# Padding small tiles so that the weights and split tiles lie at 0, the parts' tiles at 64 modulo 128 bytes

## The chip, the cores and the metric

The kernel runs on one core of a Trainium2 chip. The metric is the device time of one execution in microseconds; the median of three executions before the change is 1647.09 us (1642.84 to 1648.29).

## What is computed

A four-layer encoder over 256 tokens of 1024 features in float32. Each layer is a mixer and an MLP, both added to x; the mixers are a bidirectional state-space scan (layers 0 and 3), a dilated attention (layer 1) and a differential attention (layer 2).

```
for i in range(4):
    h = rmsnorm(x, norm_mix_g[i])
    h = (ssd_mixer, dilated_mixer, diff_mixer)[i % 3](h, ...)
    x = x + h
    x = x + square(relu(rmsnorm(x, norm_mlp_g[i]) @ w1[i])) @ w2[i]
return rmsnorm(x, final_norm_g)
```

w1 is 1024x4096, w2 4096x1024; the mixers have products of the same kind.

## The kernel before, in words

**Activations** lie as [feature, token]: x is the tile xT, 8 blocks of 128 features by 256 tokens. A product holds a 128x128 block of weights stationary in the array and moves 256 tokens past it. To get float32 accuracy from the fast float32r format, both operands are split into a rounded part and a remainder, and each product is three passes (`mm3`, lines 143, 144, 145): high weights by high x, high weights by low x, low weights by high x. A few weight chunks of the scan mixer are used whole in float32 (line 141).

**Weights** come as a stream of chunks of 128x1024 in the order in which the parts plan them: a DMA on SP's queue into raw (5 buffers), a copy on ACT into whi (line 110), a subtraction on DVE into wlo (line 112; 5 buffers each). A chunk of three passes is 24 matmuls in the MLP.

**Moving operands** are of three kinds. The norm writes x times its gains, split, into the split tiles spl (`norm_split`, lines 226 and 227; the factor of the root mean square is put in after the product). The MLP's first products ("up", banks r0 to r3) and the first units of each mixer move spl; so do the output products of the mixers, whose inputs are split into spl tiles too. The MLP's second products ("down", banks a0 to a3) move hh and hl, the split square of the first products. The other input products of the mixers move nh and nl, the split normalised x (`normalised`). Only the differential mixer's v products have it the other way: nh and nl are stationary, whi and wlo move (lines 962 to 964); the dilated mixer's v products (lines 820 to 822) likewise with 384 columns.

**Memory.** Tiles are taken from pools in the order of their first use, each at a multiple of 32 bytes of every partition: const (head, vec, cst: inputs that stay; ones; the guards of the norms), xp (xT), wp (raw, whi, wlo), sp (spl, 12 buffers), small (`ap_`: the three tiles rs_y, rs_w and rs_q of the inverse root, two buffers each, then rbc, dg, sqacc, sq), and last the pool of the part that runs (`lp`), which begins anew with each part. So an odd size in an early pool moves all that lies behind it. Start addresses modulo 128 bytes, before and after:

| tiles | before | after |
|---|---|---|
| head | 0 | 0 |
| vec | 32 | 0 |
| cst, ones | 64 | 0 |
| xT | 32 | 0 |
| raw, whi, wlo | 32 | 0 |
| spl | 32 | 0 |
| rbc, dg, sqacc, sq | 96 | 64 |
| nh, nl, nf, hh, hl | 96 | 64 |
| scan mixer: z2, cvx, cvB, cvC, bc, e, G, xt | 32 | 64 |
| dilated mixer: q, S, PT, v | 32 | 64 |
| dilated mixer: k, by head pair | 0 or 32 | 64 |
| differential mixer: q, k, S, PT | 0 | 64 |

Rows of these tiles have sizes that are multiples of 128 bytes, so that every slice that a product uses begins at the same place modulo 128 as its tile.

**Order.** The program's order is worked out ahead of the run from priorities; the engines wait for one another by semaphores. The steps of the prediction lie in `mm3`, in `rsqrt` (lines 249 to 261), in `load` (guards, lines 161 to 164), in `start` of the scan mixer (line 419: the halved gain of the skip, tile dh, read at line 620) and in the two attention mixers' small tiles (m, nm, ss, lamt, bias).

Of the kernel before, what the change touches and what calls it, by code (L numbers as in the profile page):

```python
# [10 lines left out]
F32 = mybir.dt.float32  # L11
F32R = mybir.dt.float32r
I32 = mybir.dt.int32
AF = mybir.ActivationFunctionType
ALU = mybir.AluOpType
PSUM = bass.MemoryType.PSUM
P = 128
T = 256
D = 1024
# [8 lines left out]
WARM = (8, 0, 4, 4, 4)  # L28


def classes(t):
    """Tokens j*4 + c of [.., 256] as [.., c, j]: the order of the dilated mixer."""
    return t.rearrange("p (j c) -> p c j", c=4)


class LayerPool:
    """The pool of the part that is being emitted."""
# [8 lines left out]
class Prog:  # L46
    def __init__(self, ctx, tc, aps, parts):
        self.ctx, self.tc, self.nc, self.a = ctx, tc, tc.nc, aps
        self.parts = parts
        ep = lambda name, bufs=1, **k: ctx.enter_context(tc.tile_pool(name=name, bufs=bufs, **k))  # L50
        self.const = ep("const")
        self.xp = ep("xp")
        self.wp = ep("wp")
        self.sp = ep("sp")
        self.ap_ = ep("small")
        self.lp = None
        self.dr = ep("dr", space=bass.MemoryType.DRAM)
        self.ps = ep("ps", space=PSUM)
        self.head = self.const.tile([P, aps["head"].shape[1]], F32, name="head")
        self.vec = self.const.tile([P, aps["vec"].shape[1]], F32, name="vec")  # L60
        self.cst = self.const.tile([P, aps["cst"].shape[1]], F32, name="cst")
        self.plan = []
        self.rep, self.bvec = {}, None
        self.n_dma = self.n_conv = self.n_take = self.n_done = 0
        self.chunks = {}

    @contextmanager
    def shifted(self, name):
        """Emits with the priority of a later (or earlier) place in the program."""
        n = max(self.tune[name], -self.tc.cur_priority)  # L70
        self.tc.cur_priority += n
        yield
        self.tc.cur_priority -= n

# [5 lines left out]
    def plan_chunk(self, key, ap):  # L80
        """A key that ends in "f32" is used as it is, without a split."""
        self.plan.append((key, ap))
# [44 lines left out]
    def mm2(self, out, q, kh, kl, start):  # L127
        """The product of 64 rows: q holds hi above lo, kh twice the keys' hi."""
        mm = self.nc.tensor.matmul
        mm(out, lhsT=q, rhs=kh, start=start, stop=False, skip_group_check=True)  # L130
        mm(out, lhsT=q[0:64], rhs=kl, start=False, stop=True, skip_group_check=True)  # L131
# [16 lines left out]
    def load(self, g, perm):  # L148
        """x to [feature, token] with the first gains, what the first products need ahead of the other constants."""
# [10 lines left out]
        nc.vector.memset(self.ones, 1.0)  # L160
        self.guard = {}
        for n, v in ((1, EPS / P), (D, 1.0 / D), (8 * D, 0.125 / D)):
            self.guard[n] = self.const.tile([P, 1], F32, name=f"guard{n}")
            nc.vector.memset(self.guard[n], v)
# [84 lines left out]
    def rsqrt(self, v, n):  # L249
        """1/sqrt(v) for v [128, n] (the guard within): a seed of the bits and two Newton steps, each with the factors that even its error out."""  # L250
        nc = self.nc
        t = lambda nm, dt=F32: self.ap_.tile([P, n], dt, tag=f"rs_{nm}_{n}", name=f"rs_{nm}_{n}", bufs=2)
        y, w, q = t("y"), t("w"), t("q", I32)
        nc.vector.tensor_scalar(out=q, in0=v.bitcast(I32), scalar1=-0.5, scalar2=float(0x5F1FFFF9), op0=ALU.mult, op1=ALU.add)
        cur = q.bitcast(F32)
        for a, b in ((0.703952253 * 2.38924456, 0.703952253), (1.5 * (1 + 3.17e-7), 0.5 * (1 + 3.17e-7))):
            nc.vector.scalar_tensor_tensor(out=w, in0=cur, scalar=-b, in1=cur, op0=ALU.mult, op1=ALU.mult)
            nc.vector.tensor_tensor(out=w, in0=w, in1=v, op=ALU.mult)
            nc.vector.scalar_tensor_tensor(out=y, in0=w, scalar=a, in1=cur, op0=ALU.add, op1=ALU.mult)
            cur = y  # L260
        return y

    def sums(self, bank, tiles, count):
        """bank [128 tokens, 2 blocks] = sums over the features of each [128 features, 256 tokens] over count, and eps."""
        cols = [(self.ones, self.guard[1])] + [(t, self.guard[count]) for t in tiles]
        for i, (t, v) in enumerate(cols):
            for h in range(2):
                self.nc.tensor.matmul(bank[:, h:h + 1], lhsT=t[:, 0:P] if i == 0 else t[:, h * P:(h + 1) * P], rhs=v,
                                      start=i == 0 and h == 0, stop=i == len(cols) - 1, skip_group_check=True)

    def bcast_tok(self, r, scale, bank, out):
        """r [128 tokens, 2 blocks] times scale -> out [128, 256], the same on every partition."""
# [15 lines left out]
    def normalised(self, g_mix, perm=False, keep=False):  # L288
        """x*g/rms split, all of it."""
# [87 lines left out]
    def tail_chunks(self, key, w, k0, nk):  # L377
        """The last nk row blocks of an output product, cut by columns."""
# [3 lines left out]
    def proj_tail(self, acc, key, xs, finish, first=False):  # L382
        """The last row blocks of an output product, column block by column block."""
# [14 lines left out]
    def ssd_events(self, l, finish):  # L398
        """The layer as (time, weight chunks, emitter); a unit of time is one product of two column blocks."""
# [11 lines left out]
        def start():  # L411
            self.norm_finish("a0")
            st["n"] = self.normalised(gvec("g_mix", 8 * l, 8), keep=any(n[0] != "o" for n in cfg["native"]))
            # sums of squares of the gated y, two column blocks at a time
# [3 lines left out]
            st["dh"] = lp.tile([P, 16], F32, name="dh")  # L418
            nc.vector.tensor_scalar(out=st["dh"], in0=gvec("dskip", 16 * j, 16), scalar1=0.5, scalar2=None, op0=ALU.mult)
# [3 lines left out]
        def unit(kind, c0, defer):  # L423
            """Two column blocks of in_w from column c0; -> (bank, keys)."""
# [54 lines left out]
        # dt: softplus, its logarithm, sums along the tokens within the blocks of 128  # L479
# [12 lines left out]
        def dt_post():  # L492
# [24 lines left out]
            # ln(dt): a seed of the bits and Newton steps with exp  # L517
# [8 lines left out]
        def dt_sums():  # L526
            adt, ln = st["adt"], st["ln"]
            b = self.bank("r2")
            ge, le = self.C("tri_ge"), self.C("tri_le")  # [s, s']: 1 where s >= s', s <= s'
# [24 lines left out]
        def load_rows(g, i):  # L554
            """The rows of two heads on every partition."""
# [11 lines left out]
        def cb(g):  # L567
            b = self.bank("r2")
            B, C = st["B", g], st["C", g]
            for i in range(2):  # token blocks 1, 0  # L570
# [15 lines left out]
        def gh(g, i):  # L586
            """The decayed scores of two heads, [s, l] for both directions."""
            bc, tb = st["bc", g, i], st["tb"]
            X = lambda o, i_, bias: nc.scalar.activation(out=o, in_=i_, func=AF.Exp, bias=bias)  # L589
            # blocks of 128: [s1 l0 | s1 l1 | s0 l0 | s0 l1], then the forward diagonals of token blocks 1 and 0  # L590
# [15 lines left out]
        def y(g):  # L606
# [3 lines left out]
            # two heads in turn: they hold different columns of the array  # L610
# [40 lines left out]
        def r2():  # L651
            bank = self.bank("r2")
            # the sums are of 2y
# [52 lines left out]
    def bias_vectors(self):  # L706
        """[16 heads: by k-q from -256 | the same, far ones masked | by (k-q)/4 from -64 | the same, every fourth]."""
        nc, a = self.nc, self.a
        oh = self.lp.tile([32, 1280], F32, name="oh")
        tab = self.lp.tile([32, 16], F32, name="tab")  # L710
# [13 lines left out]
    def bias_rows(self):  # L724
        """Copies of the vectors one after another, of which a slanted pattern reads Toeplitz matrices."""
# [6 lines left out]
    def slanted(self, name, h, off, dims):  # L732
        """Row h of the vectors at off - step*i for each (step, count) of dims, and so on."""
# [4 lines left out]
    def split(self, hi, lo, src, scale):  # L738
        """hi + lo = src*scale, src in PSUM or SBUF."""
# [4 lines left out]
    def dil_events(self, l, finish):  # L744
# [9 lines left out]
        def start():  # L754
# [4 lines left out]
            for i in range(2):  # L759
                st["bias", i] = lp.tile([P, 2, 514], F32, name=f"bias{i}")  # L760
# [69 lines left out]
        def scores(hp, qb):  # L830
# [10 lines left out]
            m = lp.tile([P, 4], F32, tag="m", name="m", bufs=4)  # L841
# [11 lines left out]
            nm = lp.tile([P, 6], F32, tag="nm", name="nm", bufs=4)  # L853
# [18 lines left out]
        def pv(hp, qb):  # L872
            """The two heads in turn: they hold different columns of the array."""
# [46 lines left out]
    def diff_events(self, l, finish):  # L920
# [8 lines left out]
        def start():  # L929
            self.norm_finish("a0")  # L930
            st["n"] = self.normalised(self.V("g_mix", 8 * l, 8))
            # -lambda on every partition; the gain of the head norm with its factor
            t = lp.tile([P, 6], F32, name="lamt")
# [58 lines left out]
        def scores(h, qb):  # L992
# [5 lines left out]
            m = lp.tile([P, 6], F32, tag="m", name="m", bufs=4)  # L998
# [22 lines left out]
        def pv(h):  # L1021
            b = self.bank("a3")
            pt, v = st.pop(("PT", h)), st["v", h // 2]
            m = lp.tile([P, 2], F32, tag="ss", name="ss", bufs=2)
# [59 lines left out]
    def final_tile(self, n):  # L1084
        """A feature block of x*g, transposed."""
# [42 lines left out]
    def prepare_part(self, i):  # L1128
        """Plans the weights of a part; -> its emitter."""
# [49 lines left out]
def bucket(rel):  # L1179
    """The bucket of each distance (of the shapes alone)."""  # L1180
# [6 lines left out]
def prepare(nc, ins):  # L1187
    """The arrays of the launch: the inputs, laid out, and constants of the shapes alone."""
# [73 lines left out]
```

## Time and profile before

| | |
|---|---|
| runs | 1642.84, 1648.29, 1647.09 us; median 1647.09 |
| span of the profiled execution | 1641.6 us, 1.2 us under the fastest run |
| TensorE's granted clock, mean over the span | 0.991 |
| busy: PE, weight loads, DVE, ACT, POOL | 98%, 95%, 73%, 58%, 8% |
| DMA | 299.84 MB, mean 183 GB/s |
| first MLP | about 242 to 441 us of the span |

A row of the view of a line reads: line, engine, operation, out<-in by tile names (buffer numbers left out), count, then smallest, median and largest duration in ns, then the first and last start in us. A row of the grouped view has instead the busy time in us, the mean duration in ns, and the idle time of the engine before these instructions with what ended it. A row of the timeline is start and duration in us. A matmul's record is longer than the distance to the next one's start, since matmuls overlap in the array. Some matmul records are missing from a trace, a few per cent.

### The profile page before, as it was taken

The numbers are of one execution on the slowest core, as the hardware profiler recorded it, in microseconds if no ns is written. First come the engines' busy times: TensorE is split into PE (matmuls) and PEld (weight loads), VectorE is DVE, ScalarE is ACT, GpSimd is POOL, SyncE is SP. The second block draws the span as 40 slices with busy tenths as digits, with TensorE's granted clock in tenths as the row PEclk, the third lists the DMA queues.
The fourth block names the chain that finished last, engine by engine and source line by source line (L and its number), as shares of the span: only waits on it lengthen the run. The fifth ranks groups of instructions, "written<-read, shape, count | busy, mean of one in ns | idle before, by whom it ended". The sixth has DMA issues, their size and how long they took to land.

```text
span 1641.6 us, 32376 instructions
## 1 busy us (share of the span) xinstructions
PE 1612.2 (98%) x13018; PEld 1552.6 (95%) x13018; DVE 1198.2 (73%) x1996; ACT 959.9 (58%) x1627; POOL 129.2 (8%) x116
## 2 busy tenths in 40 slices
PE   8999999999999999999999999999999999999998
PEld 7989999999999999999999999999999899899997
DVE  7999997555776666666556888755579999985554
ACT  5577865444666666655445666644455778654443
POOL 0011121000200000010000000100010231210001
PEclk9999999999999999999999999999999999999999
DMA  6677765766475555546665554566655777656651
GB/s 208 209 217 231 224 191 180 218 212 185 134 198 166 151 157 154 161 134 186 190 192 182 184 174 120 166 192 188 187 160 178 218 218 224 217 169 191 187 188 64
DMA packets 230294, 299.84 MB, mean 183 GB/s; under 512 B 16496, under 2 KB 166256, under 8 KB 230144
## 3 DMA queue, kind: packets, MB, share of 16 engines
q1 hardware_dynamic: 209552, 262.51, 52.4%
q10 hardware_dynamic: 20592, 35.27, 7.6%
q8 instruction: 102, 1.67, 0.4%
q14 instruction: 48, 0.39, 0.1%
HBM read 296.41 MB, written 3.62 MB: 183 GB/s over the span
## 4 chain that ended last, share of the span: by engine, by line
PE 79%; DVE 11%; DMA 4%; ACT 3%; issue 2%; POOL 0%; SPq 0%; DVEq 0%; ACTq 0%; POOLq 0%
PE r L143 14%; PE r L145 13%; PE r L144 13%; PE a L143 8%; PE a L145 8%; PE a L144 8%; DVE wlo L112 3%; DMA bc<-scr 2%; DMA raw<-in_ssd_in_w_dram 2%; PE r L141 1%; PE a L820 1%; PE r L614 1%; PE a L822 1%; PE a L821 1%; PE r L131 1%
## 5 line engine op out<-in xcount | busy, mean ns | idle before, releaser
L112 DVE TENSOR_TENSOR wlo<-raw,whi 128x1024 fp32r<-128x1024 f32 (+1 forms) x490 | 593.8, 1219 | 304.7 <-ACT whi L110 303.3
L110 ACT CAST whi<-raw 128x1024 fp32r<-128x1024 f32 (+1 forms) x490 | 502.6, 1032 | 458.1 <-PE r L144 237.6
L145 PE MATMUL r<-spl,wlo 128*128 128x256 f32 x1248 | 356.6, 286 | 3.7 <-DVE wlo L112 3.7
L143 PE MATMUL r<-spl,whi 128*128 128x256 f32 x1248 | 357.4, 287 | 0.5 <-ACT whi L110 0.5
L144 PE MATMUL r<-spl,whi 128*128 128x256 f32 x1248 | 357.3, 286 | 0.3 <-DVE spl L227 0.3
L143 PE MATMUL r<-nh,whi 128*128 128x256 f32 (+1 forms) x1024 | 290.1, 283 | 3.9 <-DVE cvx L469 2.4
L145 PE MATMUL r<-nh,wlo 128*128 128x256 f32 (+1 forms) x1024 | 285.0, 278 | 1.9 <-DVE wlo L112 1.9
L144 PE MATMUL r<-nl,whi 128*128 128x256 f32 (+1 forms) x1024 | 285.0, 278 | 0.0
L143 PE MATMUL a<-hh,whi 128*128 128x256 f32 x1024 | 283.2, 277 | 0.0
L144 PE MATMUL a<-hl,whi 128*128 128x256 f32 x1024 | 283.1, 276 | 0.0
L145 PE MATMUL a<-hh,wlo 128*128 128x256 f32 x1024 | 282.5, 276 | 0.0
L145 PEld LDWEIGHTS r<-spl,wlo 128*128 128x128 f32 x1248 | 242.1, 194 | 4.1 <-DVE wlo L112 3.9
L143 PEld LDWEIGHTS r<-spl,whi 128*128 128x128 f32 x1248 | 242.0, 194 | 1.1 <-ACT whi L110 0.7
L144 PEld LDWEIGHTS r<-spl,whi 128*128 128x128 f32 x1248 | 241.8, 194 | 0.9 <-DVE spl L227 0.5
L143 PEld LDWEIGHTS r<-nh,whi 128*128 128x128 f32 (+1 forms) x1024 | 192.3, 188 | 8.2 <-issue 3.6
L145 PEld LDWEIGHTS r<-nh,wlo 128*128 128x128 f32 (+1 forms) x1024 | 192.4, 188 | 2.8 <-DVE wlo L112 2.1
L144 PEld LDWEIGHTS r<-nl,whi 128*128 128x128 f32 (+1 forms) x1024 | 192.4, 188 | 0.7 <-DVE nl L300 0.2
L143 PEld LDWEIGHTS a<-hh,whi 128*128 128x128 f32 x1024 | 192.4, 188 | 0.2 <-ACT whi L110 0.2
L144 PEld LDWEIGHTS a<-hl,whi 128*128 128x128 f32 x1024 | 192.4, 188 | 0.0
L145 PEld LDWEIGHTS a<-hh,wlo 128*128 128x128 f32 x1024 | 192.2, 188 | 0.0
L240 POOL TENSOR_TENSOR sqacc<-sqacc,sq 128x256 f32<-128x256 f32 x48 | 43.5, 906 | 1129.5 <-ACT sq L238 1126.2
L589 ACT ACTIVATE e<-bc,tb 128x256 f32<-128x256 f32 (+1 forms) x256 | 95.6, 447 | 1.9 <-DVE bc L564 1.4
(250 smaller groups left out, 2421.7 us busy)
## 6 DMA issues: line engine op xcount, KB each, us to landing
raw<-in_mlp_w_dram SPq DMA_DIRECT2D x256, 512.0 KB
raw<-in_ssd_in_w_dram SPq DMA_DIRECT2D x96, 512.0 KB
bc<-scr ACTq DMA_DIRECT2D x32, 768.0 KB
raw<-in_dil_qkv_w_dram SPq DMA_DIRECT2D x48, 512.0 KB
raw<-in_ssd_out_w_dram SPq DMA_DIRECT2D x32, 512.0 KB
raw<-in_dil_qkv_w_dram SPq DMA_DIRECT2D x64, 192.0 KB
raw<-in_diff_qkv_w_dram SPq DMA_DIRECT2D x24, 512.0 KB
raw<-in_dil_out_w_dram SPq DMA_DIRECT2D x8, 512.0 KB
```

What stands on the lines that cost most here:

```text
L110: self.nc.scalar.copy(out=hi[:, :n], in_=raw[:, :n])
L112: self.nc.vector.tensor_tensor(out=lo[:, :n], in0=raw[:, :n], in1=hi[:, :n].bitcast(F32), op=ALU.subtract)
L131: mm(out, lhsT=q[0:64], rhs=kl, start=False, stop=True, skip_group_check=True)
L141: mm(out, lhsT=wh, rhs=xh, start=start, stop=stop, skip_group_check=True)
L143: mm(out, lhsT=wh, rhs=xh, start=start, stop=False, skip_group_check=True)
L144: mm(out, lhsT=wh, rhs=xl, start=False, stop=False, skip_group_check=True)
L145: mm(out, lhsT=wl, rhs=xh, start=False, stop=stop, skip_group_check=True)
L240: nc.gpsimd.tensor_tensor(out=self.sqs[0], in0=self.sqs[0], in1=sq, op=ALU.add)
L589: X = lambda o, i_, bias: nc.scalar.activation(out=o, in_=i_, func=AF.Exp, bias=bias)
L614: nc.tensor.matmul(b[(h % 2) * 64:(h % 2) * 64 + 64, n * T:(n + 1) * T], lhsT=xt[:, 1 - i, h * 64:(h + 1) * 64], rhs=G[h][:, i * T:(i + 1) ...
L820: mm(o, lhsT=nh[:, k, t], rhs=w_h, start=k == 0, stop=False)
L821: mm(o, lhsT=nh[:, k, t], rhs=w_l, start=False, stop=False)
```

## The change

- head, vec and cst get row lengths that are multiples of 32 elements (128 bytes); what is used of them stays.
- The three guards become three columns of one tile of 32 columns.
- The three tiles of the inverse root become three slices of one tile of 8 columns, with two buffers: 64 bytes in all.
- The small tiles of the attention mixers (m, nm, ss, lamt) and the table of the position bias get 32 columns each, the dilated mixer's bias tiles 528 columns instead of 514.
- The halved gain of the skip is written over its place in vec; the tile dh goes.

Comments and docstrings go too, which moves line numbers by up to 5.

```diff
+LINE = 32
+def padded(n):
+    return -(-n // LINE) * LINE
...
-        self.head = self.const.tile([P, aps["head"].shape[1]], F32, name="head")
-        self.vec = self.const.tile([P, aps["vec"].shape[1]], F32, name="vec")
-        self.cst = self.const.tile([P, aps["cst"].shape[1]], F32, name="cst")
+        self.head, self.vec, self.cst = (self.const.tile([P, padded(aps[n].shape[1])], F32, name=n)[:, :aps[n].shape[1]] for n in ("head", "vec", "cst"))
...
+        guard = self.const.tile([P, LINE], F32, name="guard")
         self.guard = {}
-        for n, v in ((1, EPS / P), (D, 1.0 / D), (8 * D, 0.125 / D)):
-            self.guard[n] = self.const.tile([P, 1], F32, name=f"guard{n}")
+        for i, (n, v) in enumerate(((1, EPS / P), (D, 1.0 / D), (8 * D, 0.125 / D))):
+            self.guard[n] = guard[:, i:i + 1]
             nc.vector.memset(self.guard[n], v)
...
-        t = lambda nm, dt=F32: self.ap_.tile([P, n], dt, tag=f"rs_{nm}_{n}", name=f"rs_{nm}_{n}", bufs=2)
-        y, w, q = t("y"), t("w"), t("q", I32)
+        t = self.ap_.tile([P, LINE // 4], F32, tag="rs", name="rs", bufs=2)
+        y, w, q = (t[:, i * n:(i + 1) * n] for i in range(3))
+        q = q.bitcast(I32)
...
-            st["dh"] = lp.tile([P, 16], F32, name="dh")
-            nc.vector.tensor_scalar(out=st["dh"], in0=gvec("dskip", 16 * j, 16), scalar1=0.5, scalar2=None, op0=ALU.mult)
+            st["dh"] = gvec("dskip", 16 * j, 16)
+            nc.vector.tensor_scalar(out=st["dh"], in0=st["dh"], scalar1=0.5, scalar2=None, op0=ALU.mult)
...
-        tab = self.lp.tile([32, 16], F32, name="tab")
+        tab = self.lp.tile([32, LINE], F32, name="tab")[:, 0:16]
...
-                st["bias", i] = lp.tile([P, 2, 514], F32, name=f"bias{i}")
+                st["bias", i] = lp.tile([P, 2, 528], F32, name=f"bias{i}")
...
-            m = lp.tile([P, 4], F32, tag="m", name="m", bufs=4)
+            m = lp.tile([P, LINE], F32, tag="m", name="m", bufs=4)
...
-            nm = lp.tile([P, 6], F32, tag="nm", name="nm", bufs=4)
+            nm = lp.tile([P, LINE], F32, tag="nm", name="nm", bufs=4)
...
-            t = lp.tile([P, 6], F32, name="lamt")
+            t = lp.tile([P, LINE], F32, name="lamt")
...
-            m = lp.tile([P, 6], F32, tag="m", name="m", bufs=4)
+            m = lp.tile([P, LINE], F32, tag="m", name="m", bufs=4)
...
-            m = lp.tile([P, 2], F32, tag="ss", name="ss", bufs=2)
+            m = lp.tile([P, LINE], F32, tag="ss", name="ss", bufs=2)[:, 0:2]
```

The sequences of PE, ACT, POOL and SP stay as they are. On DVE one instruction moves. Its place before is the end of layer 2's MLP, where the last output blocks are added to x (xT) and split (spl) for the scan mixer of layer 3; dh is that layer's halved gain of the skip:

```order
L1141 TENSOR_TENSOR xT<-xT,a_12635 128x256
L1141 TENSOR_TENSOR xT<-xT,a_12636 128x256
L419 TENSOR_SCALAR dh<-vec 128x16
L112 TENSOR_TENSOR wlo<-raw,whi 128x1024
L227 SCALAR_TENSOR_TENSOR spl<-xT,head,spl 128x256 x2
```

Its place after is at the program's start, in the first inverse root (rs) of layer 0, whose own gain is halved a few rows ahead:

```order
L259 TENSOR_SCALAR rs<-a_218 128x2
L424 TENSOR_SCALAR vec<-vec 128x16
L115 TENSOR_TENSOR wlo<-raw,whi 128x1024
L262 SCALAR_TENSOR_TENSOR rs<-rs 128x2
L115 TENSOR_TENSOR wlo<-raw,whi 128x1024
L263 TENSOR_TENSOR rs<-rs,a_218 128x2
L115 TENSOR_TENSOR wlo<-raw,whi 128x1024
L264 SCALAR_TENSOR_TENSOR rs<-rs 128x2
L424 TENSOR_SCALAR vec<-vec 128x16
L262 SCALAR_TENSOR_TENSOR rs<-rs 128x2
```

The second row with vec is the one that has moved: it needs no tile of layer 3's pool any more. In the dilated mixer a wait for POOL moves from the second to the third instruction of the scores' first row maxima.

## The prediction

> **What bounds the kernel now.** I read the page first: busy time by engine, then the chain that ended last.
>
> ```profile
> span 1641.6 us, 32376 instructions
> PE 1612.2 (98%) x13018; PEld 1552.6 (95%) x13018; DVE 1198.2 (73%) x1996; ACT 959.9 (58%) x1627; POOL 129.2 (8%) x116
> PE 79%; DVE 11%; DMA 4%; ACT 3%; issue 2%; POOL 0%; SPq 0%; DVEq 0%; ACTq 0%; POOLq 0%
> ```
>
> PE is never out of work for long: 98% busy, and 79% of the chain. Its matmuls overlap in the record, so the busy share does not say whether they run at their best rate. For that I need the distance from one start to the next, the pitch. Before that, the view of what PE waits for; its two longest entries are
>
> ```profile
> PE r L145 <- DVE wlo L112: 5.5, 2, 3.7
> PE a L268 <- POOL sqacc L240: 4.6, 3, 2.4
> ```
>
> Waits of 5 us in 1640 are not what limits PE. Next, the view of line 143 (the first of the three passes of a product; lines 144 and 145 issue the other two, equally often), with smallest, median and longest duration:
>
> ```profile
> L143 PE MATMUL r<-spl,whi x1248: 274/283/469, 10.2 to 1607.9; 128*128 128x256 f32 x179
> ...
> L143 PE MATMUL r<-nh,whi x1024: 276/276/471, 30.1 to 1420.9; 128*128 128x256 f32 x168, 128*64 128x256 f32 x3
> ...
> L143 PE MATMUL a<-hh,whi x1024: 276/276/394, 273.2 to 1632.0; 128*128 128x256 f32 x171
> ...
> L143 PE MATMUL a<-spl,whi x304: 277/283/472, 98.8 to 1448.4; 128*128 128x256 f32 x152
> ```
>
> All four have the same shape, type and stationary tiles (whi, wlo), and yet a product whose moving operand is a split tile (spl) has a median of 283 ns, one with hh or nh 276 ns. It does so in banks r and in banks a, so it is not the place in PSUM. The timeline turns this into pitch. First an "up" stage of the MLP (spl moving), first and last of 25 starts, then a "down" stage (hh moving), again 25:
>
> ```profile
> 253.00 0.28 PE L143 MATMUL r<-spl,whi 128*128 128x256 f32 x1
> ...
> 255.88 0.28 PE L143 MATMUL r<-spl,whi 128*128 128x256 f32 x1
> ```
>
> ```profile
> 896.04 0.28 PE L144 MATMUL a<-hl,whi 128*128 128x256 f32 x1
> ...
> 898.76 0.28 PE L144 MATMUL a<-hl,whi 128*128 128x256 f32 x1
> ```
>
> 2.88/24 = 120.0 ns against 2.72/24 = 113.3 ns. Duration minus pitch is 163 ns in both (283 - 120, 276 - 113), so the medians above are pitches plus a constant, and the two rates hold for whole groups.
>
> What should it be? For a few us the granted clock falls to half, and there the same spl products run at this pitch (first and tenth of ten starts):
>
> ```profile
> 1394.63 0.41 PE L145 MATMUL a<-spl,wlo 128*128 128x256 f32 x1
> ...
> 1396.55 0.41 PE L145 MATMUL a<-spl,wlo 128*128 128x256 f32 x1
> ```
>
> 1.92/9 = 213.3 ns at half clock, so the 256 columns alone would take 106.7 ns at the full one. What is above that at full clock, 6.7 ns for hh and 13.3 ns for spl, one and two sixteenths of 106.7, is not arithmetic: with PE slowed to half it vanishes. It looks like operands that don't arrive fast enough. And hh and spl differ in where they lie: modulo 128 bytes, spl and the weights are at 32, hh and nh at 96. This is what the change moves.
>
> **The change, part by part.** The split tiles and the weights go from 32 to 0 modulo 128, the parts' tiles from 32 or 96 (a few from 0) to 64. PE's sequence of instructions is the same. So PE's terms are counts times a change of pitch.
>
> Split tiles as moving operand: 3 x (1248 + 304) = 4656 matmuls at 120.0 ns. The smallest conceivable change is none. I take 113.3, the pitch that the same shape has with the same weights beside hh: 1024 bytes that begin at 32 modulo 64 touch seventeen pieces of 64 bytes, and 17/16 of 106.7 is 113.3; a second sixteenth is what spl pays beyond that. Aligned to 64, one sixteenth should go. That gives 4656 x 6.7 = 31.0 us. Of these, 4 layers x 8 stages x 96 = 3072 are the MLPs' "up" products, where PE is the bound, and pass through whole: 20.5 us. The other 1584 (10.5 us) are in mixers and output products; I give them the chain's share of PE, 79%: 8.3 us. Sum 28.8 us.
>
> For hh and nh, 3 x 2048 = 6144 matmuls at 113.3 or slightly more, the bound from below is the weight load, which runs beside each matmul and must be done before the next. Matmuls of a single column show it, four of a group before the next group starts:
>
> ```profile
> 259.84 0.58 PE L268 MATMUL a<-guard,sqacc 128*128 128x1 f32 x4
> 260.29 0.58 PE L268 MATMUL a<-guard,sq 128*128 128x1 f32 x4
> ```
>
> 0.45/4 = 112 ns with almost nothing to stream. So the piece that hh and nh too would save brings them at most 1.3 ns, 6144 x 1.3 = 8 us; I leave that to the range, as no row here shows a stream of products at the floor. If spl too went there, the whole would be 4656 x 8 + 6144 x 1.3 = 45 us; this is the low end.
>
> Can the weight stream follow? A chunk is 24 matmuls, so it must come every 2.72 us instead of 2.88. The two conversions cost, per chunk,
>
> ```profile
> L112 DVE TENSOR_TENSOR wlo<-raw,whi 128x1024 fp32r<-128x1024 f32 x456 | 562.5, 1240 | 302.5 <-ACT whi L110 301.1 <-DMA raw<-in_dil_qkv_w_dram 1.0
> L110 ACT CAST whi<-raw 128x1024 fp32r<-128x1024 f32 x456 | 475.5, 1048 | 448.0 <-PE r L144 228.1 <-PE a L144 151.2 <-DMA raw<-in_ssd_in_w_dram 18.3
> ...
> L143 PE MATMUL a<-hh,whi 128*128 128x256 f32 x1024 | 283.2, 277 | 0.0
> ```
>
> 1.24 and 1.05 us, and ACT mostly waits for PE to free a buffer. The "down" stages already take a chunk every 2.72 us with 0.0 us idle before their matmuls. The first MLP as a whole:
>
> ```profile
> 242.00:441.00 199.00, 196.09 (x1652) 0.99 0.63 192
> ```
>
> The DMA engines are 63% busy there; 3% more rate makes it 65%. So nothing is late next in the MLP.
>
> Does a tile's place alter other engines? The dilated mixer's PT lies at 32, the differential mixer's at 0; both are copies of 128x512 out of PSUM by ACT:
>
> ```profile
> L869 ACT COPY PT<-a x32: 569/587/594, 486.9 to 712.7; 128x512 f32<-128x512 f32 x32
> L1018 ACT COPY PT<-a x8: 562/586/590, 946.2 to 1018.5; 128x512 f32<-128x512 f32 x8
> ```
>
> 587 against 586 ns: nothing for ACT, and I take nothing for DVE, whose work lies under PE's anyway; a gain or loss of 1% on DVE's conversions, 6 us in all, is in time that DVE idles before them (302.5 us).
>
> The small edits: three guards and three tiles of the inverse root become one each, with the same instructions on DVE. The halved gain of the skip is written in place, so the second layer's can move from before layer 3 to the start:
>
> ```profile
> L419 DVE TENSOR_SCALAR dh<-vec x2: 164/164/165, 21.7 to 1219.0; 128x16 f32<-128x16 f32 x2
> ```
>
> 0.16 us more in the first root's chain on DVE and 0.16 less later: zero, at worst +0.2 us if PE waits for that root. The wait on POOL's fills of the dilated bias moves one DVE instruction down, behind fills long done. The DMAs carry the same bytes. All of it together: 0, bounds -0.5 to +0.5 us.
>
> The profiled span of 1641.6 us becomes 1612.8. The runs' median is 1647.1, 5.5 us above that span (the fastest run, 1642.8, is 1.2 above); with the same 5.5 the forecast is **1618 us**.
>
> **The rivals.** *No change, because the distance between the operands decides and not their place.* Moving and stationary operands are read at the same time. In the differential mixer's v products the roles are swapped: the weights, at 32, move, and nh, at 96, is stationary. The first such unit, first and last of 16 starts:
>
> ```profile
> 924.05 0.28 PE L962 MATMUL a<-whi,nh 128*128 128x256 f32 x1
> ...
> 925.75 0.28 PE L962 MATMUL a<-whi,nh 128*128 128x256 f32 x1
> ```
>
> 1.70/15 = 113.3 ns with a moving operand at 32, the place at which spl needs 120. So the moving operand's offset alone is not the cause of the second sixteenth; the distance (0 for spl, 64 here and for hh) may be. The change keeps both distances. It would leave 120 and 113.3 as they are, and the time at 1647, within 4 us. Also for this: products of 64 rows take no less with tiles at 0 (k, differential) than at 32 (q, dilated):
>
> ```profile
> L131 PE MATMUL r<-q,q x32: 379/382/382, 469.1 to 698.6; 64*128 64x256 f32 x32
> ...
> L131 PE MATMUL r<-k,q x32: 380/383/384, 935.4 to 1008.9; 64*128 64x256 f32 x32
> ```
>
> Against it: a pure conflict of two reads has no reason to leave exactly one sixteenth in every best state, and here all best states have tiles at 32 modulo 64. [...]
>
> *Slower: the mixers' second rate spreads.* Some units of nh, and later v units, run all through at another pitch, from the first start to the last of 25:
>
> ```profile
> 1240.13 0.28 PE L143 MATMUL r<-nh,whi 128*128 128x256 f32 x1
> ...
> 1242.95 0.28 PE L143 MATMUL r<-nh,whi 128*128 128x256 f32 x1
> ```
>
> 2.82/24 = 117.5 ns, with the operands where they are in the units at 113.3. So the two streams can lock in a worse phase. If at 64 against 0 this becomes the rule for hh and nh, the loss is 3072 x 4.2 for hh and at most 3072 x 4.2 for nh, some of which are there already: 13 to 26 us, 1660 to 1673. It decides from the point where spl keeps its 120; were spl to gain its 29 us, the two would cancel.
>
> **How the numbers follow.** A measurement of this kernel can tell about 0.3%, 5 us, from no change. The gain on spl in some size (1600 to 1630, likeliest 1618): 0.55. No change (1643 to 1651): 0.31. The spread of the slow rate (1660 to 1673): 0.14. Leaving out the last and the low tail, 0.8 lies between 1600 and 1654. Faster 0.55, same 0.31, slower 0.14, from the same three cases.
>
> **What would show it.** Right: in the view of line 143 the spl rows' median falls from 283 to 276 or 275 and hh's stays at 276, "up" stages step by 113 ns in the timeline, and each MLP shortens by about 5 us. The first rival is right if these medians stay at 283 and 276; the second if hh's or nh's rises toward 281. I am wrong altogether if the pitch falls and PE's waits for wlo or raw grow by as much, or if the time moves with the pitches unchanged.

## The result: slower, and the profile after

| | before | after |
|---|---|---|
| median of the runs | 1644.96 us (1641.04 to 1648.29) | 1658.91 us (1657.56 to 1660.41) |
| ratio | | 1.0086, 95% interval 1.0069 to 1.0103 |
| span of the profiled execution | 1641.6 us | 1655.9 us |

The median before is that of the three runs above and a fourth, of 1641.04 us. The kernel has become 0.9% slower: the time lies above the forecast's range and on the other side of no change. The page of the kernel after, the same three lines as of before (busy time, then the chain that ended last):

```profile
span 1655.9 us, 32377 instructions
...
PE 1632.3 (99%) x13018; PEld 1572.3 (95%) x13018; DVE 1198.0 (72%) x1996; ACT 959.3 (58%) x1627; POOL 130.0 (8%) x116
...
PE 86%; DVE 8%; ACT 2%; DMA 2%; issue 1%; POOL 0%; SPq 0%; DVEq 0%; POOLq 0%; ACTq 0%
```

Busy time on DVE, ACT and POOL is that of before within 1 us, PE's has grown by 20 us with the same 13018 matmuls, and the chain has more of PE. So nothing waits longer; the matmuls themselves are slower. The longest waits of PE after:

```profile
PE r L148 <- DVE wlo L115: 4.9, 2, 3.7
...
PE a L273 <- POOL sqacc L244: 4.2, 3, 2.4
```

They were 5.5 and 4.6 us. (Lines 143 to 145 of before are 146 to 148 here.) Which matmuls, the view of line 146 says, with smallest, median and largest duration:

```profile
L146 PE MATMUL r<-spl,whi x1248: 277/283/562, 9.8 to 1621.7; 128*128 128x256 f32 x179
...
L146 PE MATMUL r<-nh,whi x1024: 274/280/469, 30.1 to 1431.8; 128*128 128x256 f32 x168, 128*64 128x256 f32 x3
L146 PE MATMUL a<-hh,whi x1024: 276/280/383, 271.9 to 1646.3; 128*128 128x256 f32 x171
L146 PE MATMUL a<-spl,whi x304: 278/283/468, 97.9 to 1459.6; 128*128 128x256 f32 x152
```

The split tiles are where they were, 283 ns, although they are now aligned to 128 bytes. hh and nh have gone from 276 to 280. The timeline of the kernel after shows it as pitch, first an "up" and then a "down" stage, first and last of 25 starts:

```profile
264.78 0.28 PE L147 MATMUL r<-spl,whi 128*128 128x256 f32 x1
...
267.66 0.28 PE L147 MATMUL r<-spl,whi 128*128 128x256 f32 x1
...
899.83 0.28 PE L148 MATMUL a<-hh,wlo 128*128 128x256 f32 x1
...
902.66 0.28 PE L148 MATMUL a<-hh,wlo 128*128 128x256 f32 x1
```

2.88/24 = 120.0 ns as before, and 2.83/24 = 117.9 ns (starts are rounded to 10 ns; over whole stages it is 117.7) where before had 113.3. What that costs is read from the second MLP, from the first "down" stage to the seventh, six pairs of an "up" and a "down" stage of 96 matmuls each. Before and after:

```profile
750.28 0.29 PE L143 MATMUL a<-hh,whi 128*128 128x256 f32 x1
...
884.68 0.29 PE L143 MATMUL a<-hh,whi 128*128 128x256 f32 x1
```

```profile
757.29 0.28 PE L146 MATMUL a<-hh,whi 128*128 128x256 f32 x1
...
894.29 0.28 PE L146 MATMUL a<-hh,whi 128*128 128x256 f32 x1
```

134.40/6 = 22.40 us a pair before, 137.00/6 = 22.83 after. 0.43 us more in each of 4 x 8 pairs is 13.9 us, and the span has grown by 14.3. The mixers' nh products are slower too; the grouped views of before and after, busy time and mean duration:

```profile
L143 PE MATMUL r<-nh,whi 128*128 128x256 f32 (+1 forms) x1024 | 290.1, 283 | 3.9 <-DVE cvx L469 2.4
L145 PE MATMUL r<-nh,wlo 128*128 128x256 f32 (+1 forms) x1024 | 285.0, 278 | 1.9 <-DVE wlo L112 1.9
L144 PE MATMUL r<-nl,whi 128*128 128x256 f32 (+1 forms) x1024 | 285.0, 278 | 0.0
```

```profile
L146 PE MATMUL r<-nh,whi 128*128 128x256 f32 (+1 forms) x1024 | 291.5, 285 | 1.6 <-DVE cvx L474 0.8
L148 PE MATMUL r<-nh,wlo 128*128 128x256 f32 (+1 forms) x1024 | 286.1, 279 | 1.2 <-DVE wlo L115 1.2
L147 PE MATMUL r<-nl,whi 128*128 128x256 f32 (+1 forms) x1024 | 286.3, 280 | 0.0
```

The busy times sum to 863.9 instead of 860.1 us, 3.8 us more. Both together make 17.7 us, 3.4 more than the span has grown. The granted clock hides some of it: its mean was 0.991 in the profiled execution before and 0.994 in the one after. As an estimate from these figures, PE lost 1641.6 x 0.009 = 14.8 us to the lower clock before and 1655.9 x 0.006 = 9.9 us after, about 5 us less.

So the second rival of the prediction happened (the slow rate of 117.5 ns becomes the rule for hh and nh), close to its price (1660 to 1673). It did not say why. That is what the experiments are for.

### The profile page after: what moved, and what is told of

The parts are those of the page before. It is cut to its first block, busy times and chain, and to the rows that moved or that the text cites. A ratio compares the mean times of both kernels' runs of the same rounds, so it can differ in the third digit from the quotient of the medians.

```text
span 1655.9 us, 32377 instructions
## 1 busy us (share of the span) xinstructions
PE 1632.3 (99%) x13018; PEld 1572.3 (95%) x13018; DVE 1198.0 (72%) x1996; ACT 959.3 (58%) x1627; POOL 130.0 (8%) x116
## 4 chain that ended last, share of the span: by engine, by line
PE 86%; DVE 8%; ACT 2%; DMA 2%; issue 1%; POOL 0%; SPq 0%; DVEq 0%; POOLq 0%; ACTq 0%
PE r L146 15%; PE r L148 14%; PE r L147 14%; PE a L146 9%; PE a L148 8%; PE a L147 8%; PE r L144 3%; DVE wlo L115 2%; PE r L619 2%; PE a L826 1%; PE a L825 1%; PE a L827 1%; PE r L134 1%; PE a L884 1%; PE a L872 1%
## 5 line engine op out<-in xcount | busy, mean ns | idle before, releaser
L146 PE MATMUL a<-hh,whi 128*128 128x256 f32 x1024 | 287.0, 280 | 0.0
```

The source lines that it names most:

```text
L146: mm(out, lhsT=wh, rhs=xh, start=start, stop=False, skip_group_check=True)
```

## The experiments

Two theories after the result. **Place**: at 64 modulo 128 against weights at 0, products lock in the slow rate, so putting the tiles back at 32 and 96 undoes the loss. **Distance**: what counts is the number of bytes between the moving and the stationary operand. Most edits are a tile that is never used, taken ahead of a pool; this line makes 32 bytes of it:

```diff
+        ep("pad_w").tile([P, 8], F32, name="pad_w")
         self.wp = ep("wp")
```

### Matmuls alone

**micro** has no part of the computation: four stationary tiles (wa to wd) and four moving ones (ma to md) at 0, 32, 64 and 96 modulo 128, all 16 pairs, 36 matmuls of 256 columns each (RUN is 36), in three orders, the third of them twice more with a float32 matmul of 256 columns or of one ahead of each run, and with no other engine at work.

```diff
+    def run(w, m, n):
+        for i in range(n):
+            nc.tensor.matmul(bank[w][:, 0:256], lhsT=ops["w", w], rhs=ops["m", m], start=True, stop=True, skip_group_check=True)
...
+        for w, m in order:
...
+            run(w, m, RUN)
```

> Leaves the whole computation out: runs of 36 products of 128x128 by 256 columns in float32r, with the stationary tile at 0, 32, 64 or 96 bytes modulo 128 (wa to wd) and the moving tile at 0, 32, 64 or 96 (ma to md), all sixteen pairs in five orders, nothing else going on. Distance theory (what counts is the distance from the stationary to the moving operand, modulo 128): pairs of the same distance have the same median duration, about 283 ns at distance 0 and 276 or 281 at 64. Place theory (each operand's own place counts): the moving tile at 96 gives 276 beside any stationary place, at 64 about 280, at 0 and 32 about 283. If PE alone is not the cause but the other engines' traffic is, all sixteen are at 270 to 276.

Four runs of its timeline (start and length; from one start to the next are 36 pitches):

```profile
186.02 4.49 PE L36 MATMUL pd<-mc,wd 128*128 128x256 f32 x36
190.35 4.26 PE L36 MATMUL pc<-ma,wc 128*128 128x256 f32 x36
194.44 4.26 PE L36 MATMUL pd<-mb,wd 128*128 128x256 f32 x36
198.54 4.42 PE L36 MATMUL pa<-md,wa 128*128 128x256 f32 x36
```

4.33/36 = 120.3 for a pair at distance 96, then 4.09/36 = 113.6 and 4.10/36 = 113.9 ns for two at distance 64. A pair at distance 0 (ma with wa, and so on) ran at 120.0 ns in every order and at each of the four places; 113.3 came only at a distance of 64 modulo 128, and there some runs had 117.7 instead. So the rates of the kernel need no other engine, the place modulo 128 shows no part in them, and the same pair has two steady rates. The theory of place is out. But one thing remained: distance modulo 128 is the same before and after.

### Tiles put back, modulo 128

**w32s32p96** is the kernel after with the 32 bytes above: weights and split tiles at 32, the parts' tiles at 96 modulo 128, as before the change, with all its other edits.

> The changed kernel with 32 unused bytes ahead of the weights, so that weights, split tiles and parts' tiles are back at 32, 32 and 96 as before, with all other edits kept. If the places alone made the loss: 1645 us within 4, hh's median at 276, split tiles at 283. If the small edits made it (the gain written in place, one tile for the inverse root): 1659 us, whatever hh's median is.

Measured: 1662.43 us, ratio 1.0109 (1.0087 to 1.0131). The view of its first pass:

```profile
L147 PE MATMUL r<-spl,whi x1248: 277/283/561, 12.1 to 1628.1; 128*128 128x256 f32 x179
...
L147 PE MATMUL a<-hh,whi x1024: 276/280/383, 273.5 to 1652.7; 128*128 128x256 f32 x171
```

A miss for the places: every one is that of before modulo 128, and the loss stays whole, as the other branch of the expectation had it. Either the small edits cost time of their own, or what decides has a longer period than 128.

**w32s96p96** (32 bytes ahead of the weights, 64 ahead of the split tiles, 64 ahead of the parts' tiles) and **w0s32p32** (32 ahead of the split tiles, 64 ahead of the parts' tiles) give other distances: 64 for the split tiles and for hh in the one, 32 for both in the other, modulo 128.

> As w32s32p96, with 64 more unused bytes between weights and split tiles: weights at 32, split tiles and parts' tiles at 96. Distance theory: split tiles now have hh's distance of 64, their median falls from 283 to 276 (4656 x 6.7 = 31 us less at most) or to the second rate of 281 (10 us less): 1614 to 1635 us. Place theory: the moving operand at 96 gives 276, 1614 to 1620 us. If the role of the split tiles and not their place makes them slow: 283 stays, 1645 us.

> Weights at 0, split tiles and parts' tiles at 32: the distance is 32 for all, which no run has had in long stretches. Distance theory: one rate for spl, hh and nh, between 113 and 120 ns, so 1630 to 1665 us. Place theory with the moving operand at 32 as in before: 283 for all three, hh and nh lose 6144 x 6.7 = 41 us, about 1680 us.

w32s96p96: 1648.91 us, ratio 1.0035 (1.0022 to 1.0047). w0s32p32: 1653.89 us, ratio 1.0065 (1.0041 to 1.0088). Their first passes:

```profile
L149 PE MATMUL r<-spl,whi x1248: 276/279/561, 10.1 to 1612.5; 128*128 128x256 f32 x179
...
L149 PE MATMUL a<-hh,whi x1024: 276/281/386, 271.5 to 1636.6; 128*128 128x256 f32 x171
```

```profile
L148 PE MATMUL r<-spl,whi x1248: 274/278/467, 10.0 to 1617.4; 128*128 128x256 f32 x179
...
L148 PE MATMUL a<-hh,whi x1024: 277/282/387, 272.3 to 1642.2; 128*128 128x256 f32 x171
```

The first is slower than either theory had it (1614 to 1635); the second lies in the range of the distance theory, but not with one rate for all. In each, the distances of split tiles and hh are equal modulo 128, and the medians are not (279 and 281, 278 and 282). hh of the first runs some stages at 113.3 and others at 117.7; in the second neither spl, hh nor nh has a stage at 113.3. Both speak against a period of 128 too.

The addresses themselves gave the lead. From the start of whi to the start of the parts' tiles (hh, nh) there lie, before, the buffers of whi and wlo (20480 bytes each), the split tiles (24576), the inverse root's tiles (192) and the other small tiles (9216): 74944 bytes, 192 modulo 256. In the kernel after the inverse root has 64 instead of 192: 74816 bytes, **128 less, 64 modulo 256**. The table of places modulo 128 in this document cannot show that. The cause is the edit that I priced at nothing: the six 32-byte tiles of the inverse root (192 bytes) lie between the weights and the parts' tiles, and became two of 32 bytes (64). All padding ahead of the weights shifts both alike. In w32s32p96 the distance is 64 modulo 256 as well. The runs of micro already fall apart that way: by the sizes of its tiles, ma with wc and mb with wd are 192 apart modulo 256, and 6 of their 10 runs had 113.3; mc with wa and md with wb are 64 apart, and 1 of their 10 had it.

### The distance set back, and set wrong in before

**after_p128** is the kernel after, **before_p128** the kernel before, each with 128 unused bytes ahead of the parts' tiles. That moves hh by 128, from 64 to 192 in the one and from 192 to 64 in the other, and leaves every place modulo 128.

```diff
+        ep("pad_p").tile([P, 32], F32, name="pad_p")
         self.lp = None
```

> The kernel after with 128 bytes more ahead of the parts' pool, and nothing else. Places modulo 128 stay as the change sets them (weights and split tiles 0, parts 64); the distance from whi to hh goes from 64 to 192 modulo 256, which is what it is before the change. Theory of the distance modulo 256: hh and nh go back from a pitch of 117.6 to 113.3 ns, their medians to 276 ns, the split tiles stay at 283 ns, and the time goes back to that of the kernel before, 1645 us (1641 to 1650). Rival, that the place modulo 128 or the small edits made the loss: 1659 us as after, medians of hh 279 to 280.

> The kernel before with 128 bytes more ahead of the parts' pool, and nothing else: no tile changes its place modulo 128, no operation changes. Distance from whi to hh 64 instead of 192 modulo 256. Theory of the distance modulo 256: hh and nh go to 117.6 ns, medians near 280, and the time to 1659 us (1654 to 1664). Rival, place modulo 128 or the small edits: 1645 us, nothing moves.

after_p128: 1642.38 us, ratio 0.9978 (0.9966 to 0.9989). before_p128: 1660.94 us, ratio 1.0080 (1.0057 to 1.0104). First passes, in that order:

```profile
L147 PE MATMUL r<-spl,whi x1248: 277/283/468, 10.0 to 1604.2; 128*128 128x256 f32 x179
...
L147 PE MATMUL a<-hh,whi x1024: 276/276/386, 270.6 to 1628.3; 128*128 128x256 f32 x171
```

```profile
L144 PE MATMUL r<-spl,whi x1248: 277/283/561, 9.9 to 1627.8; 128*128 128x256 f32 x179
...
L144 PE MATMUL a<-hh,whi x1024: 276/280/384, 272.7 to 1652.5; 128*128 128x256 f32 x171
```

The loss is undone in the one and made in the other, in full, by 128 bytes that nobody reads. With the distance right, the change's padding and its small edits cost nothing; they gain 0.2%, and where these 3.5 us come from I did not find.

### What each distance gives

**micro2** leaves out the computation too: the moving tile at 0 to 480 bytes from the stationary one in steps of 32 (ma 0, mb 32, mc 64, ... mg 192, mh 224, mi 256 ... mp 480), 36 matmuls each (RUN), in five ways: after 24 matmuls at distance 0, after 24 at 64, after a float32 matmul of 256 columns or of one, and with the stationary tile at another place. A call of run names the bank, the stationary tile, the distance and the count; the first way is

```diff
+D = range(0, 512, 32)
...
+    for d in D:
+        run(0, 0, 0, 24)
+        run(0, 0, d, RUN)
```

> The whole computation is left out; only runs of 36 matmuls of 256 columns float32r with nothing beside them. Moving tile at distances of 0 to 480 bytes in steps of 32 from the stationary one, five ways of starting: after 24 matmuls at distance 0, after 24 at distance 64, after a float32 matmul of 256 columns, of one column, and with the stationary tile at 96. Theory of the distance modulo 256: the pitch repeats from 256 on; 0 gives 120.0 ns, 64 gives 117.7 and 192 gives 113.3 after most starts, whatever the start. Rival, that only the distance modulo 128 counts and the start chooses between two rates: 64, 192, 320 and 448 all give the same within one way of starting, and differ from one way to the other.

Of the first way, distances 64, then 192 and 256 (mi), with the 24 at 0 between:

```profile
41.98 4.41 PE L42 MATMUL pa<-mc,wa 128*128 128x256 f32 x36
46.23 1.00 PE L42 MATMUL pa<-ma,wa 128*128 128x256 f32 x7
...
70.54 4.26 PE L42 MATMUL pa<-mg,wa 128*128 128x256 f32 x36
74.64 3.02 PE L42 MATMUL pa<-ma,wa 128*128 128x256 f32 x24
...
84.63 4.48 PE L42 MATMUL pa<-mi,wa 128*128 128x256 f32 x36
88.95 1.24 PE L42 MATMUL pa<-ma,wa 128*128 128x256 f32 x9
```

4.25/36 = 118.1, 4.10/36 = 113.9, 4.32/36 = 120.0 (the first matmuls after a switch included). Steady pitch, of the second half of each run, over both periods and all five ways:

| distance modulo 256 | ns |
|---|---|
| 0 | 120.0 always |
| 32 | 116.5 to 117.8 |
| 64 | 117.7 in all 10 runs of 36; 113.3 once in a run of 24 ahead of another |
| 96 | 119.7 to 120.2 |
| 128 | 118.5 to 119.9 |
| 160 | 117.4 to 118.6 |
| 192 | 113.3 in 7 of 10, 117.8 in 3 |
| 224 | 118.2 to 118.6 |

Each row covers both periods, so over the 512 bytes tried it repeats after 256. Only 64 and 192 reached 113.3 here, 192 in 7 of 10 runs of 36 and 64 in none of 10 (once in a run of 24). Two of the three slow runs at 192 came right behind a run at 64.

**micro3** asks whether the run just before picks the rate: 24 matmuls at 64 and 12 at 192, then a few at another distance (or of one float32 column), then 36 at 192 or at 64. In the code, between is a distance and a count, and d is 192 or 64.

```diff
+            run(4, 0, 64, 24)
+            run(4, 0, 192, 12)
+            run(0, 0, *between)
+            run(b, 0, d, RUN)
```

> The whole computation is left out. 24 matmuls at distance 64 and 12 at 192 put the streams into the slow rate (117.7 ns); then a few matmuls at another distance (0, 96, 128, 160 or 224 modulo 256) or of one float32 column, then 36 at 192 or at 64. Theory that the two rates at 64 and 192 are two phases in which the streams lock, and that what ran just before picks the phase: a short stretch at distance 0 (from 1 to 8 matmuls) is enough to bring 192 to 113.3 ns, and leaves 64 at 117.7. Rival, that the rate is drawn at random with each start: the same stretch gives now the one and now the other.

Four, then eight matmuls at distance 0 (ma) ahead of the 36 at 192 (mg, bank pb):

```profile
45.29 0.63 PE L41 MATMUL pa<-ma,wa 128*128 128x256 f32 x4
45.75 4.40 PE L41 MATMUL pb<-mg,wa 128*128 128x256 f32 x36
49.99 2.99 PE L41 MATMUL pe<-mc,wa 128*128 128x256 f32 x24
...
54.23 1.12 PE L41 MATMUL pa<-ma,wa 128*128 128x256 f32 x8
55.19 4.26 PE L41 MATMUL pb<-mg,wa 128*128 128x256 f32 x36
59.29 0.99 PE L41 MATMUL pe<-mc,wa 128*128 128x256 f32 x7
```

4.24/36 = 117.8 after four, 4.10/36 = 113.9 after eight. After eight or more matmuls at any of the distances tried (0, 96, 128, 160, 224; 0 also with 24), 192 ran at 113.3 in 6 of 6 and 64 at 117.7 in 6 of 6. After one, two or four at 0, 192 was slow (3 of 3) and 64 fast in two of three; two at 224 gave what eight gave. One-column matmuls gave both at 192. The preparation itself did not hold: many of the 12 at 192 were fast already, in five of the six cases at 192 too. So the eight in the rows are the only ones that made a slow stream fast, and the four in the rows made a fast one slow. The commoner rates of the table, 113.3 at 192 and 117.7 at 64, are what a stream took behind eight or more matmuls at another distance (12 of 12 here); straight from 64 to 192, or behind four or fewer, either rate followed.

That is the kernel: the "down" stages of an MLP follow "up" stages at distance 0 (the last one follows a "down" stage). hh at 192 then has 113.3 in all 32 stages of before's profiled execution, hh at 64 has 117.7 in all 32 of the kernel after. And in w32s96p96, hh at 192 follows split tiles at 64 (both modulo 256), and has both.

One kind of product does not fit the table. In the micro kernels, and for spl, hh and nh, the moving operand lies at the higher address. In the differential mixer's v products the weights move and lie below nh, so the distance from the stationary to the moving operand is 64 before the change and 192 after. The first v unit comes straight behind split tiles at distance 0, and by the table it should have been slow before and fast after. It was the other way: 113.3 ns before (its rows are in the prediction) and 117.8 after, where every v product is slow:

```profile
L967 PE MATMUL a<-whi,nh x64: 281/281/364, 932.7 to 1009.9; 128*128 128x256 f32 x64
```

The first v units of three more kernels agree: after_p128 (64) had 113.3, w32s32p96 and before_p128 (192) had 117.8. Counted from the lower to the higher address, whichever of the two moves, all of them would fit. No micro kernel has the moving tile below the stationary one, so that is not shown.

### Split tiles at 192

If distance is all, the split tiles need not pay 120.0. **before_swap** is the kernel before with two pools in the other order, so that the split tiles too lie 192 modulo 256 from the weights; **after_swap** is the kernel after with the same, and the 128 bytes ahead of the small tiles.

```diff
-        self.sp = ep("sp")
         self.ap_ = ep("small")
+        self.sp = ep("sp")
```

> The kernel before with the pool of the split tiles taken after the small tiles instead of ahead of them, so that the split tiles lie at a distance of 192 modulo 256 from whi, as hh and nh do already; nothing else moves modulo 256. Theory of the distance modulo 256: the split tiles' pitch goes from 120.0 to 113.3 ns, the median from 283 to 276, and with 4656 matmuls of which the MLP's share passes whole, the time falls by 20 to 31 us to 1614 to 1625 us. Rival, that the rate of the split tiles comes from what they are (written by DVE in pairs just ahead of their use) and not from where they lie: medians stay at 283 and the time at 1645 us. If the slower of the two steady rates is taken: 117.6 ns, 1634 to 1638 us.

> The kernel after with 128 bytes more ahead of the small tiles, and the split tiles' pool taken behind the small tiles: split tiles and the parts' tiles all at 192 modulo 256 from the weights; the rest of the change stays. Theory: as the same swap in the kernel before, 1634 us (1630 to 1642), split tiles mostly at 276 ns, and in each MLP one rate or the other from its beginning to its end. Rival, that the padding itself costs something once the distances are right: over 1642.

before_swap: 1633.93 us, ratio 0.9945 (0.9922 to 0.9968). after_swap: 1631.91 us, ratio 0.9911 (0.9884 to 0.9937), the lowest median here, by less than the intervals tell apart. First passes, in that order:

```profile
L143 PE MATMUL r<-spl,whi x1248: 276/276/468, 10.1 to 1597.7; 128*128 128x256 f32 x179
...
L143 PE MATMUL a<-hh,whi x1024: 276/276/385, 270.9 to 1621.7; 128*128 128x256 f32 x171
```

```profile
L147 PE MATMUL r<-spl,whi x1248: 276/276/561, 10.4 to 1588.0; 128*128 128x256 f32 x179
...
L147 PE MATMUL a<-hh,whi x1024: 276/276/385, 272.7 to 1612.1; 128*128 128x256 f32 x171
```

The split tiles' median falls from 283 to 276, in before_swap with tiles at 96 modulo 128 and in after_swap at 64. The second and the third MLP of before_swap, over the same six pairs as above:

```profile
745.43 0.28 PE L143 MATMUL a<-hh,whi 128*128 128x256 f32 x1
...
875.99 0.28 PE L143 MATMUL a<-hh,whi 128*128 128x256 f32 x1
...
1052.63 0.28 PE L143 MATMUL a<-hh,whi 128*128 128x256 f32 x1
...
1188.31 0.28 PE L143 MATMUL a<-hh,whi 128*128 128x256 f32 x1
```

130.56/6 = 21.76 us a pair, and 135.68/6 = 22.61: the third MLP ran at 117.7 from its beginning to its end, up and down stages alike, 8 x 0.85 = 6.8 us. In this execution (span 1631.3 us) that is a good part of why the kernel missed my 1614 to 1625: I had let every product have 113.3. With all at 192 no stretch at another distance comes between the stages, and the slow rate can last, here through 1536 matmuls. It need not: the first MLP also began at 117.7, with 164 products, and had 113.3 from behind the norm's last product on. In the profiled execution of after_swap (span 1621.7 us) the first and the fourth MLP began slow too, but all four had 113.3 by their first "down" stage, 21.76 us a pair where nothing waited; 22.40 - 21.76 = 0.64 us in 32 pairs is 20.5 us, and its span is 19.9 under that of before. This execution was the fastest of the kernel's six (1623.7 to 1638.2 us); no trace shows the others.

**before_swap_relock** tried to renew it: eight matmuls at distance 0 at the start of the second stage of each MLP.

```diff
+                if s == 1 and j == 0:
+                    for _ in range(8):
+                        nc.tensor.matmul(b[0][:, 0:T], lhsT=wh[:, 0:P], rhs=wh[:, 0:T], start=True, stop=True, skip_group_check=True)
```

> The kernel before with the split tiles' pool behind the small tiles, and at the start of the second stage of each MLP eight matmuls of whi by whi (distance 0) into a bank whose result is then overwritten: about 8 x 0.12 = 1 us more in each of four MLPs. Theory that a stretch at distance 0 makes the next products at 192 lock at 113.3 ns: all four MLPs run at 113.3 from there on, where without it one of four in the profiled run stayed at 117.7 through 1536 matmuls (6.8 us); time 1628 to 1634 us, with less spread between runs. Rival, random draw: one or two of the MLPs still at 117.7, 1636 to 1642 us.

1632.16 us, ratio 0.9921 (0.9896 to 0.9946). All four MLPs of its profiled execution are fast (span 1626.7 us), but its ten runs spread from 1624.6 to 1643.1, as before_swap's seven do (1632.3 to 1644.5). The intervals of the two overlap, and the spread has not shrunk: inconclusive. The profiled execution tries the idea only once: its third MLP ran 162 products at 117.7 and had 113.3 right behind the eight, while the first and the fourth were at 113.3 before them. Some of the spread is the granted clock, with a mean of 0.990 to 0.992 in the three fastest runs and 0.986 to 0.987 in the three slowest. Whether an MLP stayed at 117.7 in the longer ones is open, as they left no trace.

## Why the prediction was wrong

- **What bounds the kernel, and the pitches.** Right: PE's rate, not its waits, made the difference, and 120.0, 113.3 and 117.5 ns (117.7 over whole stages) are three steady rates, seen again with nothing but matmuls. At full clock the medians were pitches plus 162 to 163 ns at all three (283 and 120.0, 280 and 117.7, 276 and 113.3).
- **"Aligned to 64, one sixteenth should go."** This step failed. The split tiles stayed at 283 ns at 0 as at 32 modulo 128. The count of 64-byte pieces was my estimate, fitted to two numbers of before, and no run shows such pieces; the 20.5 us that I saw in the MLPs are there, but came with distance 192 (after_swap), without regard to alignment. The 8.3 us of the mixers and output products did not show: after_swap's span gained 19.9 us in all.
- **"And hh and spl differ in where they lie."** They do, but I read the difference off the wrong pair of numbers. The rows that spoke against place (the v products at 113.3 ns with a moving operand at 32) stood in the prediction under the first rival, which I gave 0.31. after_p128 and before_p128 speak against place too: their tiles' places differ modulo 128, and the split tiles of both have 283 ns.
- **"The change keeps both distances"**, in the first rival. This is false, and it is why that rival fell as well: distance did decide, but modulo 256, and modulo 256 the change does not keep it. I had worked it out modulo 128 alone, since all the places were written so. For the same reason the prediction gave the v products and hh one distance, 64; from the stationary to the moving operand it is 64 for the one and 192 for the other.
- **"The small edits: zero."** As time on DVE or PE, right. As bytes, wrong: the merged tiles of the inverse root took 128 bytes out from between the weights and the parts' tiles, and that is the whole loss (before_p128).
- **hh and nh left unchanged.** The term that was missing: 0.43 us a pair, 13.9 us in the MLPs, and 3.8 us of nh's busy time beside it. The second rival had priced this at 13 to 26 us, and its row of 117.5 ns in before was the second steady rate of the very same products. I gave it 0.14, and named nothing in the change that would spread it. The worse phase of two streams by which it explained the rate was my guess: the runs show the two rates, no phase.

## What to carry to other kernels

When equal matmuls show two durations, compare the distance between the moving and the stationary operand, in bytes and modulo 256 (the period here), before their alignment; from the stationary tile up to the moving one, 192 was best here (113.3 ns in 7 of 10 runs of micro2) and 0 and 96 worst (120.0, and 119.7 to 120.2 ns), and an edit that changes the size of any tile between the two changes it. A shift that costs nothing (unused bytes, two pools in another order) is the test, in both directions: 128 bytes took hh's median from 280 to 276 ns in after_p128 and from 276 to 280 in before_p128. Look also at the sequence: at 192 a run had 117.8 ns behind four matmuls at 0 and 113.9 behind eight (micro3).

## What the runs showed of the hardware that was not expected

- A float32r product of 128 rows by 256 columns had a pitch between 113.3 and 120.2 ns by the distance of its operands, with a period of 256 bytes over the 512 tried and no other engine at work (micro2); at 64 and 192 also by what ran just before (micro3).
- At distances 64 and 192 there were two steady rates, 113.3 and 117.7 ns; the slow one lasted through 1536 matmuls (third MLP of before_swap). After eight or more matmuls at another distance 192 had the fast and 64 the slow one in 12 of 12 cases; after four or fewer at distance 0 it was the other way in 5 of 6 (micro3). Why 64 and 192 differ is open, and so is why the v products, with the moving operand at the lower address, have it the other way round.
